# Softmax units bound for a DMA transpose keep their exponentials in PSUM and are split from there

## The chip, the cores and the metric

The kernel runs on one core of a Trainium2 chip. The metric is the device time of one execution in microseconds (us). Five engines have queues of their own: TensorE (PE in the profile; PEld is its weight load), VectorE (DVE), ScalarE (ACT), GpSimd (POOL) and SyncE (SP), which here issues all DMA transfers.

## The reference

Two residual layers on x of 1024 tokens by 1024 columns. Each layer norms x, projects it once, runs three mixers on the parts, multiplies each by its SiLU gate, projects the concatenation back and adds it to x.

```python
for layer in range(2):
    h = rms_norm(x, ln_g[layer])
    if layer % 2 == 0:
        u = h @ even_w_in[0]
        y1 = mla_mixer(...) * silu(a_gate)      # 8 heads, causal softmax over 1024 keys
        y2 = nsa_mixer(...) * silu(b_gate)      # 8 heads; compressed, all earlier and last 512 keys
    else:
        u = h @ odd_w_in[0]
        y1 = dsa_mixer(...) * silu(c_gate)      # 8 heads; softmax over the 256 keys an indexer picks
        y2 = mlstm_mixer(...) * silu(d_gate)    # matrix memory, no softmax
    y_m = mem_xattn(...)                        # 4 heads, softmax over 256 memory slots
    x = x + concat(y1, y2, y_m * silu(m_gate)) @ w_out[layer]
```

Every softmax is exp(s - max s), its sum, and the product with V divided by that sum.

## The kernel before

**The planner.** No engine's order is written out by hand. The kernel is recorded as a list of operations on virtual tiles. `places` gives each operation a due key from the segment that it belongs to (the table `SEG`: start and end key) and makes one order by key, as far as dependencies and room for tiles allow. `order` then deals the operations out to the engines by list scheduling with modelled costs (`time_of`), modelled hand-over times (`LAT`) and the room in four SBUF pools and eight PSUM banks (`LIMITS`: "pg" 30 pages of 4 KB, "hp" 32 of 2 KB, "B" 8 banks). An operation recorded with alternatives (`rec.flex`) goes to the engine that would finish it first by the model. The order that comes out is fixed in the program; the chip keeps it, engine by engine.

A segment's key counts only against other work that is ready at the same time: `mem1` (the second memory attention) has keys far below its neighbours and still waits for the projection that makes its queries.

**The attention units.** `attention` cuts each mixer's softmax into units of one tile of 128 queries and one to four heads: up to 512 score columns in one unit, or one head where a head alone has more. A unit goes through these steps:

- `u_S`: matmuls write the scores to one or two PSUM banks (two beyond 512 columns). DVE takes the row maximum, negated, into `nm`. Then ln 2048 (`lnp`) is added to `nm`, on DVE or POOL. For the masked dsa units one DVE instruction adds the mask, writes the sum to an SBUF page `smask` and returns the maximum; negation and ln 2048 are one more DVE instruction.
- `u_exp`: one ACT instruction for each head reads the scores (PSUM, or `smask`), adds `nm`, takes the exponential, writes fp32 to an SBUF page `P` and sums the row into `rs`. The row's largest value is so 2048.
- Then one of two ways to the transposed fp16 pair that PV takes. A unit with `turn` is split in SBUF by `u_split`: high half `PS[:,0]` = fp16(P), a flex copy for ACT or DVE; low half `PS[:,1]` = P - high, a flex subtraction for DVE or POOL. One DMA transpose then moves both halves to `PT`. A unit without `turn` is transposed by TensorE in fp32 (`psum<-cst,P`), and ACT copies the high half and DVE subtracts the low half out of PSUM (`u_T`, `u_lo`).
- `u_PV`: three matmuls for each block of 128 keys, high and low halves of P and V.

`TURN` sets which units turn: half of mla and nsa, all of mem, three quarters of dsa.

**Stages of the profiled run.** 0 to 300 us: start and even projections. 300 to 850: mla, nsa and the first memory attention among the rest of the projections. 850 to 1200: output projection of layer 0, odd projections, the search for the top 256 keys. 1200 to 1365: second memory attention, mLSTM and the end of the search. 1365 to 1549: dsa and the last output projections.

All recorded instructions show line L558 (the place where `issue` emits them), so the profile is read by tile names.

Of the kernel before, what the change touches and what calls it, by code (L numbers as in the profile page):

```python
# [8 lines left out]
F = mybir.dt.float32  # L9
R = mybir.dt.float32r  # L10
BF = mybir.dt.bfloat16
H = mybir.dt.float16
I32 = mybir.dt.int32
AF = mybir.ActivationFunctionType
OP = mybir.AluOpType
# [618 lines left out]
NEG = -1e30  # L634
EPS = 1e-6
NT = 8
LNP = float(np.float32(11 * np.log(2.0)))
SPLIT = 3
LIMITS = {"pg": 30, "hp": 32, "t8": 32, "t32": 8, "B": 8}

# [21 lines left out]
def shape_constants():  # L662
# [8 lines left out]
    for i in range(NT):  # L671
# [5 lines left out]
    return c  # L677


SEG = dict(setup=(-540.765888, -490.733443), norm=(12.964708, 132.050679), e_agate=(31.455813, 704.234339), kv0=(167.224773,  # L680
           345.119047), late=(175.636113, 461.177491), nsak=(275.848244, 1055.795764), q1=(476.701035, 603.438676),
           cmp=(484.672636, 639.334256), nsav=(624.336051, 851.116142), e_kv1=(652.6, 653.6), e_lat=(663.1, 841.289575),
           e_bgate=(688.806149, 749.106149), q0=(713.750502, 956.450502), kv1=(725, 935.4), e_bq=(743.2, 988.9), e_mq=(762.470888,
           932.2), e_kv2=(794.4, 841.5), nsa=(850.7, 1310.2), tab1=(897.605545, 1585.900938), mla0=(911.5, 1001.5), mla1=(952.8,
           1035.2), mem1=(1004.344435, 1330.229828), oA0=(1007.9, 1178.4), mkv0=(1037.7, 1137.062), mem0=(1060.581418, 1262.6),
           oBM0=(1118.8, 1360.2), o_idx=(1297.169979, 1412.178903), topk0=(1312.341201, 1905.3), o_og1=(1334.12618, 1624.221757),
           o_cgate=(1379.576354, 1777.449577), topk1=(1430.809671, 1885.899198), o_og0=(1492.923662, 1808.788497),
           o_mq=(1651.070557, 1759.482667), o_cq=(1677.868104, 1840.650339), o_dqk=(1707.761464, 1804.647378), mlstm=(1753.080505,
           2015.6), o_dv=(1790.7, 1900.9), mkv1=(1795.03316, 1858.78446), oBM1=(1913.5, 2201.9), cv=(1942.975868, 2132.206114),
           dsa=(1984.716978, 2256.916978), oA1=(2154.023358, 2441.25515))  # L690


LOENG = "GV"
UNIT = 512
NMENG = "GV"
# [8 lines left out]
class Trunk:  # L704
# [88 lines left out]
    def setup(self):  # L793
        V, S, G, T, Q, A = self.V, self.S, self.G, self.T, self.Q, self.A
        cst = self.const([128, C_F32], F, "cst")
        Q.dma_start(cst, A["cst"][:, 0:C_F32])
        self.cst = cst
        self.idf = cst[:, C_ID:C_ID + 128]
        self.gcol = gcol = self.const([128, GCOL], F, "gcol")
        Q.dma_start(gcol, A["cols"])  # L800
        self.nhalf = self.const([128, 32], F, "nhalf")
        V.memset(self.nhalf, -0.5)
        self.lnp = self.const([128, 4], F, "lnp")
        V.memset(self.lnp, LNP)
        self.half = self.const([128, 8], F, "half")
        V.memset(self.half, 0.5)
        self.ones = self.const([128, 128], F, "ones")
        V.memset(self.ones, 1.0)
        self.gmax = self.const([128, 6], F, "gmax")
        self.gcols = {}  # L810
        cols = self.tiny(6, F, "gcm")
        for j, (nm, o, n) in enumerate((("ln0", 0, 8), ("ln1", 8, 8), ("mem0", 16, 8), ("mem1", 24, 8), ("qlat", 32, 2), ("kvlat", 34, 1))):
            self.gcols[nm] = (gcol[:, o:o + n], self.gmax[:, j:j + 1])
            V.tensor_reduce(out=cols[:, j:j + 1], in_=gcol[:, o:o + n], axis=AX.X, op=OP.max, apply_absolute_value=True)
        self.gcols[None] = (None, 1.0)
        gm = self.spread(cols, 6)
        V.tensor_copy(self.gmax, gm)
        V.tensor_tensor(out=self.gmax, in0=self.gmax, in1=self.gmax, op=OP.mult)
# [288 lines left out]
    def v_scale(self, views, nh, c=1):  # L1107

        V = self.V
        m = self.tiny(nh, F, "vm")  # L1110
        for n, v in enumerate(views):
            P = v.shape[0]
            dst = m if n == 0 else self.tiny(nh, F, "vm2")
            if n == 0 and P < 128:
                V.memset(m, 0.0)
            V.tensor_reduce(out=dst[0:P], in_=v, axis=AX.X, op=OP.max, apply_absolute_value=True)
            if n:
                V.tensor_tensor(out=m[0:P], in0=m[0:P], in1=dst[0:P], op=OP.max)
        e = self.tile([128, 3, 8], F, "t32", "vsc")
        V.tensor_scalar(e[:, 0, 0:nh], self.spread(m, nh), 1e-30, None, op0=OP.max)  # L1120
        V.tensor_scalar(e[:, 0, 0:nh].bitcast(I32), e[:, 0, 0:nh].bitcast(I32), 0x7F800000, None, op0=OP.bitwise_and)
        V.tensor_scalar(e[:, 1, 0:nh].bitcast(I32), e[:, 0, 0:nh].bitcast(I32), -1.0, float(268 << 23), op0=OP.mult, op1=OP.add)
        V.tensor_scalar(e[:, 2, 0:nh].bitcast(I32), e[:, 0, 0:nh].bitcast(I32), float((14 + c) << 23), None, op0=OP.subtract)
        return e[:, 1, 0:nh], e[:, 2, 0:nh]

    def v_split(self, v, scale, hi, lo):
# [35 lines left out]
    def u_S(self, u):  # L1162
        T, V = self.T, self.V
        g = u["grp"]
        n, st = u["n"], u["st"]
        per = len(u["heads"])
        s = u["s"] = self.psS(1 if per * st <= 512 and n <= 512 else 2)
        k = min(len(u["heads"]), max(1, 512 // st))
        banks = [[], []]
        for j, h in enumerate(u["heads"]):  # L1170
            for x, (c0, c1) in enumerate(self.cuts(n)):
                b, o = (x, 0) if n > 512 else (j // k, j % k * st)
# [15 lines left out]
                T.matmul(o, l, r, start=(x == 0), stop=(x == len(mm) - 1))  # L1188
        nm = u["nm"] = self.tiny(per, F, "nm")
        if g.get("addmask") is not None:  # L1190
            sm = u["sm"] = self.page("smask")
            for j in range(per):
                V.tensor_tensor_reduce(out=self.like(sm[:, j * n:(j + 1) * n], n), in0=self.head(u, j),
                                       in1=self.like(g["addmask"], n), scale=1.0,
                                       scalar=-3e38, op0=OP.add, op1=OP.max, accum_out=nm[:, j:j + 1])
            V.tensor_scalar(nm, nm, -1.0, LNP, op0=OP.mult, op1=OP.add)
            return
        elif n > 512:
            V.tensor_reduce(out=nm, in_=self.span(s, n).unsqueeze(1), axis=AX.XY, op=OP.max, negate=True)
        elif k > 1:  # L1200
            nb = per // k
            sv = s[:, :, 0:k * st].rearrange("p b (h c) -> p b h c", h=k)[:, :, :, 0:n]
            V.tensor_reduce(out=nm.rearrange("p (b h) -> p b h", b=nb), in_=sv, axis=AX.X, op=OP.max, negate=True)
        else:
            V.tensor_reduce(out=nm, in_=s[:, :, 0:n], axis=AX.X, op=OP.max, negate=True)
        self.tt(nm, nm, self.lnp[:, 0:per], OP.add, NMENG)

    def head(self, u, j):
        n, st, s = u["n"], u["st"], u["s"]
# [3 lines left out]
        return s[:, j // k, j % k * st:j % k * st + n]  # L1213

    def u_exp(self, u):
        g = u["grp"]
        n, st = u["n"], u["st"]
        p = u["p"] = self.page("P", [128, n * len(u["heads"])])
        for j, h in enumerate(u["heads"]):
            src = self.like(u["sm"][:, j * n:(j + 1) * n], n) if "sm" in u else self.head(u, j)  # L1220
            self.S.activation(self.like(p[:, j * n:(j + 1) * n], n), src, AF.Exp, bias=u["nm"][:, j:j + 1], scale=1.0,
                              accum_out=g["rs"][:, h:h + 1])

    def u_split(self, u):

        if not u["turn"]:
            return
        n = u["n"] * len(u["heads"])
        ps = u["ps"] = self.page("PS", [128, 2, n], H)
        p = u["p"][:, 0:n]  # L1230
        self.copy(ps[:, 0], p)
        self.tt(ps[:, 1], p, ps[:, 0], OP.subtract, LOENG)

    def u_T(self, u):
        n = u["n"] * len(u["heads"])
        nb = n // 128
        pt = u["pt"] = self.page("PT", [128, 2, nb, 128], H)
        if u["turn"]:
            self.turn(pt.rearrange("p f k c -> p (f k) c"), u["ps"].rearrange("p f c -> p (f c)"))
            return  # L1240
        p = u["p"]
        u["tt"] = []
        for b0 in range(0, nb, 4):
            b1 = min(nb, b0 + 4)
            t = self.psT()
            for b in range(b0, b1):
                self.T.transpose(t[:, 128 * (b - b0):128 * (b - b0) + 128], p[:, 128 * b:128 * b + 128], self.idf)
            self.S.activation(pt[:, 0, b0:b1].rearrange("p k c -> p (k c)"), t[:, 0:128 * (b1 - b0)], AF.Copy)
            u["tt"].append((b0, b1, t))

    def u_lo(self, u):
        pt = u["pt"]
        for b0, b1, t in u.get("tt", []):
            f = lambda x: pt[:, x, b0:b1].rearrange("p k c -> p (k c)")
            self.V.tensor_tensor(out=f(1), in0=t[:, 0:128 * (b1 - b0)], in1=f(0), op=OP.subtract)

    def u_PV(self, u):
        g, pt, T = u["grp"], u["pt"], self.T
# [1207 lines left out]
```

## Time and profile before

| | |
|---|---|
| median of 3 runs | 1545.11 us (1543.31 to 1551.86) |
| the profiled execution | 1550.77 us, its span 1548.9 us |
| mean granted TensorE clock | 0.956 of full speed |
| busy in the span | PE 1392.3, DVE 1378.1, ACT 1048.5, POOL 419.7 us |

Busy time sums the durations of an engine's instructions. PE's are modelled and overlap, so its share is an upper reading. The median lies 5.66 us under the profiled execution, which has 1.9 us outside its span.

### The profile page before, as it was taken

Reading aid. Unit: us, or ns where it says so; the run is one execution under the profiler, and the core shown is the slowest. Engines: PE = TensorE matmul, PEld = TensorE weight load, DVE = VectorE, ACT = ScalarE, POOL = GpSimd, SP = SyncE. Lnnn points to the kernel's source line nnn. Section 1 sums busy time; section 2 is a strip of 40 time slices with the busy share of each in tenths; the row PEclk is TensorE's granted clock in tenths of the full one; section 3 lists DMA queues with packets and bytes.
Section 4 is the critical chain, followed back from the end, with each engine's and each line's share of the span. In section 5 each row is a group of like instructions: output and inputs, shape, how many; then the busy total and the mean of one; then the engine's idle time right before and its main releaser. Section 6 shows DMA issues by size and latency. Waiting matters only on the chain.

```text
span 1548.9 us, 30286 instructions
## 1 busy us (share of the span) xinstructions
PE 1392.3 (90%) x10407; PEld 797.4 (51%) x10407; DVE 1378.1 (89%) x3813; ACT 1048.5 (68%) x2498; POOL 419.7 (27%) x527
## 2 busy tenths in 40 slices
PE   4999999978888778969889999999989879998988
PEld 1445546545556655546555554444444455656544
DVE  7765989999999988899889999999999989798994
ACT  7633775576767777786686689999875763466650
POOL 1311244546633242243323200003330212121220
PEclk9999999989999999989999999999998867699999
DMA  9826522367496798979997413201431285299995
GB/s 289 195 75 172 158 71 93 88 150 159 100 179 114 156 183 236 220 138 205 209 235 174 108 48 131 81 25 51 123 109 51 62 181 133 74 207 235 212 232 162
DMA packets 441850, 225.49 MB, mean 146 GB/s; under 512 B 378080, under 2 KB 404320, under 8 KB 441696
## 3 DMA queue, kind: packets, MB, share of 16 engines
q1 hardware_dynamic: 441696, 223.57, 61.0%
q8 instruction: 81, 1.33, 0.4%
q14 instruction: 73, 0.60, 0.1%
HBM read 83.61 MB, written 46.66 MB: 84 GB/s over the span
## 4 chain that ended last, share of the span: by engine, by line
PE 31%; DVE 13%; DMA 4%; issue 2%; ACT 1%; POOL 0%; SPq 0%; ACTq 0%; DVEq 0%
PE psum L558 31%; DMA PT<-PS 3%; DVE tkj L558 1%; DVE nm L558 1%; DVE smask L558 1%; DVE PS L558 1%; DVE wl L558 1%; DVE tkp L558 1%; DVE osp L558 1%; DVE row L558 1%; DVE tke L558 0%; DVE PT L558 0%; DMA oT<-osp 0%; DMA gate<-gate_d 0%; DVE x L558 0%
## 5 line engine op out<-in xcount | busy, mean ns | idle before, releaser
L558 PE MATMUL psum<-wl,hT 128*128 128x512 f16 (+3 forms) x2880 | 669.0, 374 | 11.2 <-DMA hT<-nh 4.0
L558 PEld LDWEIGHTS <-hT 128*128 128x128 f16 x2880 | 280.2, 99 | 315.9 <-issue 36.4
L558 PE MATMUL psum<-wl,oT 128*128 128x512 f16 x960 | 266.3, 382 | 5.7 <-DVE mixM L558 1.9
L558 PEld LDWEIGHTS <-PT 128*128 128x128 f16 x3792 | 223.7, 102 | 92.0 <-DMA PT<-PS 50.7
L558 ACT ACTIVATE P<-psum,nm 128x256 f32<-128x256 f32 (+8 forms) x336 | 191.8, 582 | 90.9 <-POOL nm L558 37.2
L558 POOL TENSOR_TENSOR ms<-ms,nhalf 128x4 f32<-128x4 f32 (+3 forms) x105 | 114.2, 1097 | 430.6 <-DVE ms L558 261.4
L558 PE MATMUL psum<-nv,PT 128*128 128x64 f16 x1584 | 174.8, 195 | 19.6 <-DMA PT<-PS 16.7
L558 DVE TENSOR_REDUCE nm<-psum 128x2 f32<-128x512 f32 (+8 forms) x216 | 162.9, 764 | 16.7 <-PE psum L558 16.4
L558 ACT ACTIVATE tkj<-tkj 128x512 bf16<-128x512 bf16 (+5 forms) x192 | 149.9, 783 | 17.2 <-DVE tkj L558 13.0
L558 PEld LDWEIGHTS <-oT 128*128 128x128 f16 x960 | 93.2, 99 | 102.5 <-issue 6.9
L558 DVE TENSOR_TENSOR PS<-P,PS 128x512 f16<-128x512 f32 (+6 forms) x138 | 116.8, 849 | 1.3 <-ACT PS L558 1.2
L558 PE MATMUL psum<-cst,P 128*128 128x128 f32 x502 | 102.8, 292 | 13.2 <-ACT P L558 9.1
L558 PEld LDWEIGHTS <-qf 128*128 128x128 f16 x832 | 77.6, 103 | 49.3 <-issue 15.2
L558 ACT ACTIVATE wj<-wr 128x1024 bf16<-128x1024 f32 (+4 forms) x76 | 77.7, 1024 | 27.8 <-DMA wr<-w_out 16.7
L558 ACT ACTIVATE PT<-psum 128x512 f16<-128x512 f32 (+3 forms) x160 | 76.5, 504 | 29.3 <-PE psum L558 21.7
L558 PE MATMUL psum<-nkst,qf 128*128 128x320 f16 (+5 forms) x384 | 90.2, 319 | 5.8 <-DVE PT L558 2.5
L558 DVE TENSOR_TENSOR wl<-wr,wl 128x1024 f16<-128x1024 f32 (+3 forms) x79 | 93.7, 1190 | 1.8 <-ACT wl L558 1.6
L558 DVE TENSOR_TENSOR PT<-psum,PT 128x512 f16<-128x512 f32 (+3 forms) x160 | 88.1, 566 | 2.0 <-ACT PT L558 1.7
L558 PE MATMUL psum<-cvp,PT 128*128 128x64 f16 x864 | 70.9, 195 | 13.1 <-DMA PT<-PS 10.1
L558 PEld LDWEIGHTS psum<-cst,P 128*128 128x128 f32 x502 | 65.7, 142 | 32.0 <-ACT P L558 13.6
L558 PE MATMUL psum<-vp,PT 128*128 128x64 f16 x864 | 65.3, 197 | 11.9 <-DMA PT<-PS 6.7
L558 POOL TENSOR_TENSOR nm<-nm,lnp 128x1 f32<-128x1 f32 (+2 forms) x116 | 30.6, 265 | 149.1 <-DVE nm L558 133.2
(494 smaller groups left out, 2894.0 us busy)
## 6 DMA issues: line engine op xcount, KB each, us to landing
wr<-even_w_in SPq DMA_DIRECT2D x20, 512.0 KB, 6.0
wr<-w_out SPq DMA_DIRECT2D x20, 512.0 KB, 5.1
wr<-odd_w_in SPq DMA_DIRECT2D x20, 512.0 KB, 4.9
gate<-gate_d SPq DMA_DIRECT2D x32, 256.0 KB, 3.8
gate_d<-gu SPq DMA_DIRECT2D x24, 256.0 KB, 2.2
qa_d<-mqT SPq DMA_DIRECT2D x16, 384.0 KB, 2.4
xt<-x SPq DMA_DIRECT2D x8, 512.0 KB, 10.3
x<-x SPq DMA_DIRECT2D x8, 512.0 KB, 4.7
```

The costliest lines, as they stand in the source:

```text
L558: r = getattr(engines[o.eng], meth)(*[res(a) for a in args], **{k: res(v) for k, v in kw.items()})
```

## The change

1. `lnp` and the addition of ln 2048 to `nm` are gone, so exponentials reach 1 and not 2048. The factor comes back as `PSCALE` = 2048 where the fp16 halves are made: `scale=PSCALE` on the high copy, and a `scalar_tensor_tensor` (in0 x 2048 - high) for the low half. For units without `turn` these are the same two instructions out of PSUM with a factor in them. The constants of `v_scale` undo the factor in the row sums.
2. A unit with `turn` has no page `P`: ACT writes the exponentials over the scores in PSUM, and both halves are made from there. The low half can then only be DVE's (`sub` with a factor names DVE alone). The high copy stays a choice of ACT and DVE.
3. The masked dsa scores go back into their PSUM banks and not to `smask`; this page is gone for all dsa units with a mask.
4. Of the 42 segments of the `SEG` table 35 have new keys. Those that move most (start to end key): `nsak` 276-1056 to 515-835, `kv0` 167-345 to 79-407, `late` 176-461 to 108-589, `norm` 13-132 to 34-47, `cmp` 485-639 to 385-672, `o_mq` 1651-1759 to 1595-1695, `o_cq` 1678-1841 to 1736-1892, `cv` 1943-2132 to 1846-2069, `oBM1` 1914-2202 to 1962-2217, `mem1` 1004-1330 to -818-279.

```diff
-LNP = float(np.float32(11 * np.log(2.0)))
+PSCALE = 2048.0
...
-        self.lnp = self.const([128, 4], F, "lnp")
-        V.memset(self.lnp, LNP)
...
-            sm = u["sm"] = self.page("smask")
             for j in range(per):
-                V.tensor_tensor_reduce(out=self.like(sm[:, j * n:(j + 1) * n], n), in0=self.head(u, j),
-                                       in1=self.like(g["addmask"], n), scale=1.0,
+                V.tensor_tensor_reduce(out=self.head(u, j), in0=self.head(u, j), in1=self.like(g["addmask"], n), scale=1.0,
                                        scalar=-3e38, op0=OP.add, op1=OP.max, accum_out=nm[:, j:j + 1])
-            V.tensor_scalar(nm, nm, -1.0, LNP, op0=OP.mult, op1=OP.add)
-            return
+            V.tensor_scalar(nm, nm, -1.0, None, op0=OP.mult)
...
-        self.tt(nm, nm, self.lnp[:, 0:per], OP.add, NMENG)
...
     def u_exp(self, u):
-        p = u["p"] = self.page("P", [128, n * len(u["heads"])])
+        if not u["turn"]:
+            u["p"] = self.page("P", [128, n * len(u["heads"])])
         for j, h in enumerate(u["heads"]):
-            src = self.like(u["sm"][:, j * n:(j + 1) * n], n) if "sm" in u else self.head(u, j)
-            self.S.activation(self.like(p[:, j * n:(j + 1) * n], n), src, AF.Exp, bias=u["nm"][:, j:j + 1], scale=1.0,
-                              accum_out=g["rs"][:, h:h + 1])
+            src = self.head(u, j)
+            dst = src if u["turn"] else self.like(u["p"][:, j * n:(j + 1) * n], n)
+            self.S.activation(dst, src, AF.Exp, bias=u["nm"][:, j:j + 1], scale=1.0, accum_out=g["rs"][:, h:h + 1])
...
     def u_split(self, u):
-        p = u["p"][:, 0:n]
-        self.copy(ps[:, 0], p)
-        self.tt(ps[:, 1], p, ps[:, 0], OP.subtract, LOENG)
+        n, per = u["n"], len(u["heads"])
+        ps = u["ps"] = self.page("PS", [128, 2, n * per], H)
+        k = min(per, max(1, 512 // u["st"]))
+        if n > 512 or per == 1:
+            src, f = self.head(u, 0), lambda x: self.like(ps[:, x], n)
+        else:
+            src = u["s"][:, :, 0:k * u["st"]].rearrange("p b (h c) -> p b h c", h=k)[:, :, :, 0:n]
+            f = lambda x: ps[:, x].rearrange("p (b h c) -> p b h c", b=per // k, h=k)
+        self.copy(f(0), src, scale=PSCALE)
+        self.sub(f(1), src, f(0), scale=PSCALE)
...
-            self.S.activation(pt[:, 0, b0:b1].rearrange("p k c -> p (k c)"), t[:, 0:128 * (b1 - b0)], AF.Copy)
+            self.S.activation(pt[:, 0, b0:b1].rearrange("p k c -> p (k c)"), t[:, 0:128 * (b1 - b0)], AF.Copy, scale=PSCALE)
...
-            self.V.tensor_tensor(out=f(1), in0=t[:, 0:128 * (b1 - b0)], in1=f(0), op=OP.subtract)
+            self.sub(f(1), t[:, 0:128 * (b1 - b0)], f(0), scale=PSCALE)
```

## Rows read from the trace of the kernel before

**Rows 1.** Windows: us, busy us (instructions) by engine, granted clock, DMA share, GB/s

```profile
300.00:850.00 550.00, 464.86 (x5036) 309.79 (x5034) 512.16 (x1248) 398.19 (x1039) 210.15 (x306) 0.97 0.82 173
850.00:1200.00 350.00, 344.40 (x1638) 165.16 (x1636) 334.97 (x905) 293.61 (x643) 58.13 (x54) 0.98 0.28 83
1200.00:1365.00 165.00, 143.43 (x780) 86.18 (x779) 145.45 (x413) 90.72 (x250) 30.09 (x29) 0.76 0.47 117
1365.00:1549.00 184.00, 165.00 (x1558) 95.72 (x1557) 151.22 (x412) 91.73 (x203) 31.04 (x31) 0.98 0.94 210
```

**Rows 2.** The page, chain that ended last, share of the span by engine

```profile
PE 31%; DVE 13%; DMA 4%; issue 2%; ACT 1%; POOL 0%; SPq 0%; ACTq 0%; DVEq 0%
```

**Rows 3.** Waits of PE, 300 to 850 us: total us, times, longest us

```profile
PE psum L558 <- DMA PT<-PS: 28.4, 19, 5.0
PE psum L558 <- ACT P L558: 19.4, 26, 2.2
PE psum L558 <- DVE PT L558: 16.0, 22, 1.7
```

**Rows 4.** Waits of ACT, 300 to 850 us

```profile
ACT P L558 <- POOL nm L558: 32.3, 28, 3.2
```

**Rows 5.** Groups by shape: the additions to nm on DVE (busy us, mean ns)

```profile
L558 DVE TENSOR_TENSOR nm<-nm,lnp 128x1 f32<-128x1 f32 x61 | 11.2, 184 | 0.2
L558 DVE TENSOR_TENSOR nm<-nm,lnp 128x2 f32<-128x2 f32 x29 | 4.5, 154 | 0.0
L558 DVE TENSOR_TENSOR nm<-nm,lnp 128x4 f32<-128x4 f32 x10 | 2.0, 201 | 0.0
```

**Rows 6.** Timeline around 448 us: start us, us, instruction

```profile
447.36 0.95 DVE L558 TENSOR_REDUCE nm<-psum 128x1 f32<-128x768 f32 x1
...
448.39 0.19 POOL L558 TENSOR_TENSOR nm<-nm,lnp 128x1 f32<-128x1 f32 x1 [2.37 <-DVE nm L558]
...
448.61 0.90 ACT L558 ACTIVATE P<-psum,nm 128x768 f32<-128x768 f32 x1
...
449.63 0.84 ACT L558 ACTIVATE PS<-P 128x768 f16<-128x768 f32 x1
...
450.92 1.65 POOL L558 TENSOR_TENSOR PS<-P,PS 128x768 f16<-128x768 f32 x1
```

**Rows 7.** Windows of tile PS alone: busy us (instructions) DVE, ACT, POOL

```profile
300.00:850.00 550.00, 107.24 (x146) 31.02 (x47) 20.86 (x15) 0.97 0.82 173
1200.00:1365.00 165.00, 16.18 (x29) 5.03 (x8) 0.00 (x0) 0.76 0.47 117
1365.00:1549.00 184.00, 40.61 (x57) 9.41 (x12) 10.95 (x7) 0.98 0.94 210
```

**Rows 8.** Windows of tile nm alone: busy us (instructions) DVE, ACT, POOL

```profile
300.00:850.00 550.00, 161.93 (x276) 185.72 (x576) 29.44 (x112) 0.97 0.82 173
1200.00:1365.00 165.00, 15.69 (x39) 20.31 (x80) 0.39 (x2) 0.76 0.47 117
```

**Rows 9.** The page's groups: the low halves on DVE (busy us, mean ns)

```profile
L558 DVE TENSOR_TENSOR PS<-P,PS 128x512 f16<-128x512 f32 (+6 forms) x138 | 116.8, 849 | 1.3 <-ACT PS L558 1.2
```

**Rows 10.** Groups by shape on DVE, 512 columns (mean ns)

```profile
L558 DVE TENSOR_TENSOR PS<-P,PS 128x512 f16<-128x512 f32 x54 | 41.2, 766 | 0.6 <-ACT PS L558 0.5
L558 DVE TENSOR_TENSOR PT<-psum,PT 128x512 f16<-128x512 f32 x92 | 62.0, 682 | 1.4 <-ACT PT L558 1.3
L558 DVE CAST PS<-P 128x512 f16<-128x512 f32 x34 | 16.1, 474 | 0.5 <-ACT P L558 0.5
L558 DVE TENSOR_SCALAR gu<-psum,winv 128x512 f32<-128x512 f32 x8 | 6.0, 744 | 0.0
```

**Rows 11.** Groups by shape on ACT, 512 columns (mean ns)

```profile
L558 ACT ACTIVATE PT<-psum 128x512 f16<-128x512 f32 x92 | 54.2, 595 | 24.1 <-PE psum L558 17.3 <-DVE PS L558 3.7 <-DMA PT<-PS 2.4
L558 ACT ACTIVATE PS<-P 128x512 f16<-128x512 f32 x28 | 17.8, 635 | 0.4
```

**Rows 12.** Windows of tile smask alone: busy us (instructions) DVE, ACT

```profile
1365.00:1549.00 184.00, 41.22 (x47) 45.83 (x96) 0.98 0.94 210
```

More of the change, by code (lines that the diff above doesn't have):

```diff
@@ L677, in shape_constants @@
     return c
[L680 to L690, printed above, removed]
@@ new lines @@
+SEG = dict(setup=(-887.176746, -575.014179), mem1=(-818.104608, 279.148712), e_agate=(30.064605, 726.188487), norm=(33.814806,
+           46.567053), kv0=(79.294457, 406.744216), late=(107.887518, 589.489146), cmp=(384.926552, 672.131649), q1=(486.699749,
+           566.879955), nsak=(515.461903, 834.75308), nsav=(539.37667, 851.116142), e_kv1=(647.207588, 648.207588), e_lat=(663.1,
+           841.289575), q0=(716.011325, 958.711325), e_bgate=(717.414855, 765.602334), kv1=(721.080648, 931.480648), e_bq=(743.2,
+           988.9), e_mq=(765.062608, 934.79172), e_kv2=(784.700952, 841.5), nsa=(850.7, 1310.2), tab1=(907.178297, 1568.867316),
+           mla0=(911.5, 1001.5), mla1=(949.844544, 1032.244544), oA0=(1017.297313, 1145.595371), mkv0=(1037.7, 1137.062),
+           mem0=(1060.562837, 1262.240461), oBM0=(1119.643991, 1371.691747), o_idx=(1293.212411, 1403.388382), topk0=(1314.820916,
+           1927.025474), o_og1=(1332.958304, 1623.288011), o_cgate=(1393.498171, 1809.325093), topk1=(1431.703909, 1887.435987),
+           o_og0=(1537.324563, 1830.06217), o_mq=(1595.039309, 1695.130732), o_dqk=(1707.756033, 1804.641946), o_cq=(1735.958173,
+           1892.235555), mlstm=(1752.857474, 2015.6), o_dv=(1790.7, 1900.9), mkv1=(1795.03316, 1858.78446), cv=(1845.919745,
+           2068.562291), oBM1=(1961.877043, 2217.498363), dsa=(1968.250395, 2289.566052), oA1=(2185.072731, 2442.45093))
@@ L1119, in v_scale @@
         e = self.tile([128, 3, 8], F, "t32", "vsc")
-        V.tensor_scalar(e[:, 0, 0:nh], self.spread(m, nh), 1e-30, None, op0=OP.max)
+        V.tensor_scalar(e[:, 0, 0:nh], self.spread(m, nh), 1e-29, None, op0=OP.max)
         V.tensor_scalar(e[:, 0, 0:nh].bitcast(I32), e[:, 0, 0:nh].bitcast(I32), 0x7F800000, None, op0=OP.bitwise_and)
         V.tensor_scalar(e[:, 1, 0:nh].bitcast(I32), e[:, 0, 0:nh].bitcast(I32), -1.0, float(268 << 23), op0=OP.mult, op1=OP.add)
-        V.tensor_scalar(e[:, 2, 0:nh].bitcast(I32), e[:, 0, 0:nh].bitcast(I32), float((14 + c) << 23), None, op0=OP.subtract)
+        V.tensor_scalar(e[:, 2, 0:nh].bitcast(I32), e[:, 0, 0:nh].bitcast(I32), float((25 + c) << 23), None, op0=OP.subtract)
         return e[:, 1, 0:nh], e[:, 2, 0:nh]
@@ L1216, in u_exp @@
         g = u["grp"]
-        n, st = u["n"], u["st"]
-        p = u["p"] = self.page("P", [128, n * len(u["heads"])])
+        n = u["n"]
+        if not u["turn"]:
+            u["p"] = self.page("P", [128, n * len(u["heads"])])
         for j, h in enumerate(u["heads"]):
-            src = self.like(u["sm"][:, j * n:(j + 1) * n], n) if "sm" in u else self.head(u, j)
-            self.S.activation(self.like(p[:, j * n:(j + 1) * n], n), src, AF.Exp, bias=u["nm"][:, j:j + 1], scale=1.0,
-                              accum_out=g["rs"][:, h:h + 1])
+            src = self.head(u, j)
+            dst = src if u["turn"] else self.like(u["p"][:, j * n:(j + 1) * n], n)
+            self.S.activation(dst, src, AF.Exp, bias=u["nm"][:, j:j + 1], scale=1.0, accum_out=g["rs"][:, h:h + 1])
     def u_split(self, u):
@@ L1227, in u_split @@
             return
-        n = u["n"] * len(u["heads"])
-        ps = u["ps"] = self.page("PS", [128, 2, n], H)
-        p = u["p"][:, 0:n]
-        self.copy(ps[:, 0], p)
-        self.tt(ps[:, 1], p, ps[:, 0], OP.subtract, LOENG)
+        n, per = u["n"], len(u["heads"])
[8 more added lines that the diff above has]
+        self.sub(f(1), src, f(0), scale=PSCALE)
     def u_T(self, u):
```

## The prediction

> **What bounds the kernel now.** I read the windows by stage first. In the attention stage, 300 to 850 us, DVE is busy 512.2 of 550 us (93%), PE 464.9 (85%), ACT 398.2 (72%) and the DMA engines 0.82 of the time; from 850 to 1200 PE is busy 344.4 of 350; from 1200 to 1365 the granted clock is only 0.76 with DVE at 88%; in the dsa stage DVE is at 82%, PE at 90%, the DMA engines at 0.94 [rows 1]. So the change lands in three stages and in none does one engine do everything. The chain of work that ended last says the same: 31% of the span on PE, 13% on DVE, 4% on DMA [rows 2]. In the attention stage PE waits 28.4 us for transposed pairs, 19.4 us for exponentials and 16.0 us for low halves out of PSUM [rows 3]. The reader is to see that DVE is the fullest there, but that a third of what PE waits for is the transpose behind it.
>
> **1. The addition of ln 2048 goes.** On DVE 61 + 29 + 10 = 100 additions take 11.2 + 4.5 + 2.0 = 17.7 us, 0.177 us each [rows 5]. In the attention stage tile nm has 276 instructions on DVE and 112 on POOL; one addition goes with each maximum, so DVE has (276 - 112)/2 = 82 additions: -14.5 us. From 1200 to 1365 it has (39 - 2)/2, some 18: -3.3 us [rows 8]. The dsa mask units keep their one small instruction. Beside the work a hand-over goes: around 448 us the maximum ends at 448.31, POOL's addition runs to 448.58, the exponential starts at 448.61 [rows 6], so a unit loses 0.3 us there and without POOL perhaps 0.1. ACT ended 28 waits on such an addition, 32.3 us in all [rows 4], but most of each is the maximum that came late. At 0.2 us for the 26 times that PE waited for an exponential [rows 3] the hand-over is worth 5 us at most; I take -2.
>
> **2. The low half moves to PSUM and wholly to DVE.** 138 on DVE took 116.8 us, 849 ns each [rows 9]. At 512 columns the same subtraction is 766 ns from SBUF and 682 ns from PSUM (the low half after a TensorE transpose) [rows 10]. That row has no factor; the third operation of the new instruction runs in the same pass, and the nearest row with a factor from PSUM, a copy with a pointer, is 744 ns, which is the upper end. I take 849 x 682/766 = 756 ns. POOL's share comes over.
>
> **3. The high copy.** From SBUF DVE needs 474 ns at 512 columns, ACT 635; from PSUM ACT needs 595 [rows 10, 11] and DVE, by the subtraction's row, 682. DVE was the cheaper place and becomes the dearer one, so the planner will give ACT more. In the attention stage tile PS has 146 instructions on DVE, 47 on ACT, 15 on POOL: 208, so 104 units, with 104 - 15 = 89 low halves and 57 copies on DVE [rows 7]. Before, DVE had 57 of 104; I take a third, 35, after. The Trainium skill, "VectorE: DVE Perf Modes", section "Why PSUM operands drop a tier", says that a PSUM operand costs a DVE copy its double rate in fp32; the trace agrees, 474 against 682 ns. Its section "Rules for kernel authors" goes on that many operations on a matmul's output want a copy to SBUF first, which is what the old kernel did: by that rule the change loses (rival D).
>
> **DVE by stage.** Attention: 104 low halves and 35 copies x 0.756 = 105.1 us against 107.2 now [rows 7]; with the additions -16.6. Bounds: all 57 copies stay, 161 x 0.756 = 121.7, sum 0.0; all leave, 78.6, sum -43. From 1200 to 1365: 37 instructions, 18.5 units of 512 columns, 18.5 + 6 at 0.682 = 16.7 against 16.2; with the additions -2.8. Dsa: (57 + 12 + 7)/2 = 38 units, now 40.6 us on DVE [rows 7]. They are wider: the masking of one such unit out of PSUM takes 41.22/47 = 0.877 us [rows 12], so 38 + 13 operations are 44.7 us: +4.1. Bounds: no copy on DVE, 33.3, -7.3; the present 57 - 31 = 26 stay, 56.1, +15.5.
>
> **ACT and POOL.** In the attention stage ACT takes 22 copies more, at 31.02/47 = 0.66 less 0.04 us: +14, to 75% busy; that has room. POOL loses its 20.9 + 29.4 us [rows 7, 8] and was the bound nowhere.
>
> **4. Writing to PSUM.** No row has ACT or DVE write there. For ACT's exponentials and DVE's masking I take the present price; the bounds are the two sides of what another place of a source makes, 40 ns on ACT and 84 ns on DVE at 512 columns [rows 10, 11]: within 4 us of DVE work for the 47 masked heads, and ACT has room. The masked exponentials read PSUM in place of SBUF, which by the same 40 ns saves 2 us of ACT.
>
> **5. Banks are held longer.** A turned unit now gives its scores' bank back when the exponential ends, at 449.51 in the example; afterwards when the low half is made. The copy there ran from 449.63 to 450.47 and the subtraction (POOL's, begun at 450.92) needs some 0.9 us on DVE [rows 6]: some 2 us longer, in two banks beyond 512 columns. 104 units x 2 us x 1.5 banks = 312 of 8 x 550 = 4400 bank-us, 7%. Below: nothing, if the planner finds another bank; above: rival C. I take +1 us. The Trainium skill, "ScalarE: Activation LUTs", section "Step-by-step: what each stage is for", calls PSUM the faster destination for ScalarE, useful only if TensorE does not need most of it. No row here shows such a write; the caveat is rival C.
>
> **6. Pages.** Up to 160 `P` pages and 48 masks are no longer allocated; that lets later units start earlier. No price shows; I count nothing, and the upside is in rival B.
>
> **7. The new keys.** Each moved segment issues the same instructions and DMAs; what changes is whom they are queued in front of, SP's transfers included. `kv0`, `late` and `norm` bring weight and table loads forward behind the first x tiles; `cv` brings its transpose of keys and three DVE instructions ahead of `oBM1`; `o_mq` passes `o_cq`, so the second memory attention can begin earlier, and cq's stores wait. From 850 to 1200 PE is at 344.4 of 350 us, so no order there can win more than 5.6. From 1200 to 1365 there is more: 143.4 us of PE work at clock 0.76 [rows 1] would be some 109 at full clock, so up to -34. A wrong order costs by the same measure. `mem1` was far ahead of its neighbours already and its new key changes nothing. I take 0 in the middle, +-15.
>
> **The sum.** Of 16.6 us less DVE work in the attention stage I let three fifths, 10, reach the end, since PE's 28.4 us for transposes stay. Hand-over -2; 1200 to 1365 -1; dsa +2 (half of 4.1, as DVE is at 82%); banks +1: -10 us. The profiled execution's 1550.77 us would be 1540.8; it lies 5.66 us above the median of the runs, so against 1545.11 I predict 1535.
>
> **The rivals.**
> A. Nothing changes: PE and the transposes set the end. For it: the chain, and PE's longest wait [rows 2, 3]. Against: DVE at 93%. Within 5 us of 1545.
> B. More than forecast: units run ahead on the freed pages, half of PE's 19.4 us for exponentials goes (-10), and the new order wins a third of the 34 us at the low clock (-11). With the -10: 1514.
> C. Banks: score matmuls wait for a bank until the low half is made. 10 us over 104 units is 0.1 us a unit; from there the gain is gone. At 0.25 us a unit it is +26 - 10: 1561. For it: 7% more bank time and PE's 16.0 us for low halves out of PSUM; against: the order is planned with the banks.
> D. The copies stay on DVE: 0 in the attention stage, half of 15.5 in dsa: 1553.
>
> **Chances.** Forecast 0.42 (its own range 1527 to 1541), A 0.20, B 0.16, C 0.12, D 0.10. Less than 0.5% (7.7 us) can't be told from no change. Faster by more: 0.36 of the forecast's 0.42, all of B, a trace of A: 0.53. Slower: C, half of D, a little of A: 0.19. The same: 0.28. From 1508 to 1560 leaves out about half of B's faster end and two thirds of C, under 2 in 10 together.
>
> **What would show it.** No nm addition on POOL; the exponential a hand-over behind the maximum. PS rows: 160 low halves on DVE near 756 ns, under 60 copies on DVE, over 100 on ACT. DVE in the attention stage some 15 us lower. Under C, PE waits in front of score matmuls (psum<-Kn, nkst, ckst) for DVE PS or ACT PS, where none stand now. Wrong it would be if the clock between 1200 and 1365 moves far from 0.76, which the keys can do and no term here sizes, or if DVE's idle time grows as much as its work shrinks.

## The result, and the profile after

Over four runs the new kernel's median is 1530.78 us (1522.73 to 1536.33); before, beside it, 1545.78. The ratio is 0.9891, 95% interval 0.9858 to 0.9924: 1.1% faster, where the prediction gave 1535. The profiled execution took 1530.51 us, span 1528.7; before, 1548.9. So the two traces differ by 20.2 us, 5 more than the medians.

Windows by stage, new kernel (columns as in [rows 1]):

```profile
300.00:850.00 550.00, 475.17 (x5088) 313.78 (x5087) 508.38 (x1162) 414.17 (x1072) 171.87 (x205) 0.97 0.79 176
850.00:1200.00 350.00, 338.80 (x1623) 163.94 (x1620) 338.21 (x901) 293.82 (x645) 43.70 (x42) 0.98 0.27 80
1200.00:1365.00 165.00, 148.18 (x874) 90.03 (x873) 154.87 (x440) 94.10 (x273) 44.82 (x46) 0.79 0.54 126
```

The attention stage has 10 us more of PE's work in the same 550 us, and DVE is nearly as full as before (508.38 against 512.16 us), though tiles nm and PS alone cost it 18 us less: work moved forward into the stage. ACT's 16 us more are the high copies that it took over (48.18 against 31.02 us on tile PS). The chain that ended last reaches back to 44.94 us here. That of [rows 2] reaches back only to 753.71 us, so its shares add up to about half of the span, and the two can't be compared:

```profile
PE 47%; DVE 33%; DMA 7%; issue 5%; ACT 3%; POOL 1%; SPq 0%; DVEq 0%; POOLq 0%; ACTq 0%
```

Windows of tile PS (first three lines: attention, 1200 to 1365, dsa; DVE, then ACT), and of tile nm (last line, attention), which answer to [rows 7, 8]:

```profile
300.00:850.00 550.00, 103.42 (x136) 48.18 (x72) 0.97 0.79 176
1200.00:1365.00 165.00, 22.85 (x37) 10.86 (x19) 0.79 0.54 126
1365.00:1529.00 164.00, 31.93 (x33) 18.91 (x23) 1.00 0.94 224
...
300.00:850.00 550.00, 147.67 (x194) 189.95 (x576) 0.97 0.79 176
```

POOL is gone from both tiles. Tile PS by operation (count: shortest/median/longest ns, over the whole run):

```profile
L558 DVE SCALAR_TENSOR_TENSOR PS<-psum,PS x160: 409/682/1225, 324.6 to 1493.2; 128x512 f16<-128x512 f32 x62, 128x640 f16<-128x640 f32 x30, 128x384 f16<-128x384 f32 x18, 128x768 f16<-128x768 f32 x14
...
L558 ACT ACTIVATE PS<-psum x114: 374/643/1046, 320.2 to 1491.9; 128x512 f16<-128x512 f32 x40, 128x640 f16<-128x640 f32 x19, 128x384 f16<-128x384 f32 x15, 128x768 f16<-128x768 f32 x11
L558 DVE TENSOR_SCALAR PS<-psum x46: 418/682/1224, 337.1 to 1464.9; 128x512 f16<-128x512 f32 x22, 128x640 f16<-128x640 f32 x11, 128x384 f16<-128x384 f32 x3, 128x896 f16<-128x896 f32 x3
```

Waits of PE, 300 to 850 us, to be held against [rows 3]:

```profile
PE psum L558 <- DVE PS L558: 21.3, 24, 3.2
PE psum L558 <- DMA PT<-PS: 15.8, 16, 3.3
PE psum L558 <- DVE PT L558: 9.9, 15, 1.8
PE psum L558 <- ACT P L558: 5.9, 10, 1.8
```

The first line is new: matmuls that wait until a bank's low half is made. The other three fell from 28.4 + 19.4 + 16.0 = 63.8 us to 31.6; with the new one it is 52.9.

**Where the 20.2 us arose.** The tile views give the start of the last matmul of a kind. The last nsa product with V (`psum<-nv,PT`) starts at 845.6 us before and at 838.2 after: 7.4 us. The first exponential came at 308.7 and comes at 304.9, so 3.8 of these lie ahead of it and 3.6 behind it. But before, an addition on POOL stood in front of that exponential, so part of the change's own gain lies ahead of this landmark. The first row maximum starts at 304.6 and 303.5: counted from it, 1.1 lie ahead of the attention and 6.3 in it. The last projection matmul (`psum<-wl,hT`) starts at 1299.9 and 1281.9: a further 10.6 us between the two landmarks. From there to the end it is 249.0 and 246.8: 2.2 us. Windows of the middle stretch, before and then after:

```profile
845.60:1299.90 454.30, 429.74 (x2176) 214.31 (x2174) 430.96 (x1158) 355.66 (x815) 76.82 (x74) 0.94 0.33 93
```

```profile
838.20:1281.90 443.70, 420.14 (x2180) 210.82 (x2179) 427.77 (x1133) 352.60 (x814) 71.88 (x76) 0.96 0.34 95
```

PE issues the same matmuls there, and its idle time is 24.6 and 23.6 us. 9.6 of the 10.6 us are matmul time, at a granted clock of 0.94 against 0.96. Slices of 10 us show where. Before:

```profile
1150.00:1160.00 10.00, 6.17 (x32) 3.06 (x29) 10.00 (x24) 9.95 (x21) 1.58 (x2) 0.98 0.67 182
1160.00:1170.00 10.00, 9.69 (x22) 3.68 (x23) 9.66 (x16) 6.70 (x17) 0.21 (x1) 0.51 0.47 105
1170.00:1180.00 10.00, 10.00 (x23) 2.83 (x21) 9.64 (x10) 3.27 (x4) 0.00 (x0) 0.66 0.00 0
...
1250.00:1260.00 10.00, 7.21 (x66) 4.97 (x65) 10.00 (x28) 8.86 (x31) 0.74 (x3) 0.50 1.02 199
...
1270.00:1280.00 10.00, 10.00 (x61) 6.31 (x60) 7.26 (x26) 3.91 (x9) 1.01 (x1) 0.50 0.90 306
```

PE was busy 6.17 of 10 us, and in the next slice it has 1.2 GHz (0.51) and gets through 22 matmuls where the slices around have some 50. Between 1100 us and the last projection matmul four slices of before are at 0.57 or less; the new kernel has none there (its next is at 0.50, from 1290 us, behind that matmul), the lowest being this one:

```profile
1230.00:1240.00 10.00, 5.77 (x39) 3.65 (x39) 10.00 (x22) 8.14 (x32) 0.60 (x3) 0.59 0.95 160
```

So half of the difference between the two traces lies where few turned units run. The experiments ask what belongs to the code and what to the order of its work.

### The profile page after: what moved, and what is told of

Same layout as the page of the kernel before. It is cut to its first block, busy times and chain, and to the rows that moved or that the text cites. A ratio compares the mean times of both kernels' runs of the same rounds, so it can differ in the third digit from the quotient of the medians.

```text
span 1528.7 us, 29963 instructions
## 1 busy us (share of the span) xinstructions
PE 1386.7 (91%) x10407; PEld 793.7 (52%) x10407; DVE 1375.7 (90%) x3683; ACT 1066.5 (70%) x2527; POOL 375.4 (25%) x413
## 4 chain that ended last, share of the span: by engine, by line
PE 47%; DVE 33%; DMA 7%; issue 5%; ACT 3%; POOL 1%; SPq 0%; DVEq 0%; POOLq 0%; ACTq 0%
PE psum L558 47%; DMA PT<-PS 6%; DVE nm L558 5%; DVE PS L558 4%; DVE tkj L558 3%; DVE wl L558 3%; DVE PT L558 2%; DVE cy L558 1%; DVE score L558 1%; DVE psum L558 1%; POOL ms L558 1%; DVE mixB L558 1%; DMA xp_d<-x 1%; DVE qs L558 1%; DVE wr L558 1%
## 5 line engine op out<-in xcount | busy, mean ns | idle before, releaser
L558 PE MATMUL psum<-wl,oT 128*128 128x512 f16 x960 | 274.2, 386 | 8.6 <-DVE PS L558 3.2
L558 ACT ACTIVATE tkj<-tkj 128x640 bf16<-128x640 bf16 (+5 forms) x192 | 149.8, 782 | 39.5 <-DVE tkj L558 30.9
L558 ACT ACTIVATE psum<-psum,nm 128x256 f32<-128x256 f32 (+8 forms) x234 | 137.1, 590 | 54.3 <-DVE nm L558 39.9
L558 DVE SCALAR_TENSOR_TENSOR PS<-psum,PS 128x512 f16<-128x512 f32 (+6 forms) x160 | 123.7, 782 | 2.2 <-ACT PS L558 2.0
L558 ACT ACTIVATE P<-psum,nm 128x64 f32<-128x64 f32 (+8 forms) x150 | 92.5, 625 | 37.6 <-DVE nm L558 27.4
L558 DVE SCALAR_TENSOR_TENSOR PT<-psum,PT 128x512 f16<-128x512 f32 (+3 forms) x160 | 87.9, 566 | 9.0 <-ACT PT L558 8.6
L558 ACT ACTIVATE wj<-wr 128x1024 bf16<-128x1024 f32 (+6 forms) x78 | 79.2, 1016 | 19.2 <-DMA wr<-even_w_in 7.5
L558 DVE TENSOR_TENSOR wl<-wr,wl 128x1024 f16<-128x1024 f32 (+4 forms) x75 | 90.8, 1219 | 1.3 <-ACT wl L558 1.1
L558 PE MATMUL psum<-cvp,PT 128*128 128x64 f16 x864 | 81.6, 193 | 7.2 <-DMA PT<-PS 6.5
L558 ACT ACTIVATE PS<-psum 128x512 f16<-128x512 f32 (+6 forms) x114 | 78.0, 686 | 2.0 <-PE psum L558 0.3
```

The lines of the kernel that those rows point to most:

```text
L558: r = getattr(engines[o.eng], meth)(*[res(a) for a in args], **{k: res(v) for k, v in kw.items()})
```

## The experiments

Runs are compared by their ratio to the kernel before, measured beside them. A difference of two such ratios, times 1545.8, is given in us; the new kernel's own ratio, 0.9891, is uncertain by 5 us.

**Keys and code apart.** e1 is the old code with the new table, e2 the new code with the old one.

```diff
-SEG = dict(setup=(-541..., ...), ...)   # e1: in the old code
+SEG = dict(setup=(-887.176746, -575.014179), mem1=(-818.104608, 279.148712), ...)
```

> The kernel before with nothing changed but the key table of the new one. Theory A (the code makes the gain: less DVE work and no hand-over through POOL): ratio to the kernel before 0.997 to 1.003. Theory B (the key table makes it): 0.985 to 0.992, and most of it after 850 us, where the new kernel's last hT matmul comes 18 us earlier while its attention stage (first exponential to last nv product) is only 3.6 us shorter. Theory C (the order that the planner happens to find makes it): anywhere from 0.99 to 1.01.

> The new kernel with the old key table. Theory A: 0.987 to 0.993, all of the gain. Theory B: 0.997 to 1.005. If both parts add up, the product of this ratio and that of the run with the new keys alone is 0.989.

e1: 1589.52 us, ratio 1.0284 (1.0251 to 1.0317). e2: 1559.81, 1.0105 (1.0076 to 1.0135). Each is slower than both kernels, so neither part alone makes the old kernel faster.

**Keys moved by nothing that means anything.** If a table fits its own code, a small random shift should cost. In e3 (old code) and e4 (new code) each pair of keys is shifted by a random amount of at most 1, on a scale of some 3,000.

```diff
-nsa=(850.7, 1310.2), ...
+nsa=(851.590541, 1311.090541), ...   # e3; each segment its own shift
```

> The kernel before, each segment's key pair shifted by a random amount within 1 (of some 2400): no meaning in it, so it measures what an arbitrary new order is worth. Theories A and B: 0.997 to 1.003. Theory C: a shift as large as the gain itself, 0.5% or more either way.

> The new kernel with its key pairs shifted in the same way within 1. Theories A and B: 0.986 to 0.992 as the new kernel itself. Theory C: it loses half of the gain or more, 0.994 or above.

e3: 1573.67 us, 1.0187 (1.0163 to 1.0210): 29 us slower than before. e4: 1559.07, 1.0094 (1.0071 to 1.0118): 31 us slower than the new kernel. Both tables stand on a narrow peak. An order found for one code costs about as much on another as one found for none, so e1 and e2 say little by themselves about keys or code: each lost its own peak.

**The code on keys chosen for neither.** e5 is the new code on e3's keys. A second shift gives the pair e9 (old code) and e10 (new code).

> The new code with the shifted old keys of the run before_keys_shifted (1573.7 us), so that neither code has a table sought out for it. If the code is worth what it is worth between the two tuned kernels, 10 to 20 us less: ratio to the kernel before 1.005 to 1.012. If the code is worth nothing and the two tables differ by luck: 1.014 to 1.022. If more than between the tuned kernels: under 1.005.

> Before's code; each old pair of keys moved by a second random amount of at most 1. With e10 it is a second pair on keys chosen for neither code (the first was e3 and e5, 1573.7 and 1570.5 us). Theory 1 (what a key table is worth to its own code is larger than what the change of code is worth): slower than before by 15 to 45 us, 1560 to 1590. Rival (the 28 us of e3 were bad luck with one table): within 8 us of 1546.

> The new code with the keys of e9. Theory 1 as in e3 and e5: the two differ by under 10 us in either direction. Rival (the code is worth its 15 us on any keys, and the first pair hid it): 12 us or more below e9.

| keys | old code | new code | difference |
|---|---|---|---|
| first shift: e3, e5 | 1.0187 | 1.0170 (1.0133 to 1.0208) | -0.2%, 3 us |
| second shift: e9, e10 | 1.0243 (1.0205 to 1.0281) | 1.0136 (1.0093 to 1.0178) | -1.1%, 17 us |
| last nsa product with V, e3, e5 | 869.8 us | 862.1 us | -7.7 us |
| the same, e9, e10 | 872.5 us | 853.5 us | -19.0 us |

e9 repeats what a shift costs, 38 us. The pairs differ by 3 and 17 us, some 10 us with an uncertainty nearly as large. What I held after the first pair, that the code is worth less than 10 us, fell with the second. The attention stage is what holds up: on both tables it ends earlier with the new code, by 8 and 19 us. Counted from the first row maximum (306.8 and 305.8 us in e3 and e5, 304.7 and 303.7 in e9 and e10) it is 6.7 and 18.0 us shorter. In the first pair some 5 us of that were given back later.

All untuned orders together say more than the two pairs. The new code has four of them (e2, e4, e5 and e10), with ratios from 1.0094 to 1.0170 and a mean of 1.0126. The old code has three (e1, e3 and e9), from 1.0187 to 1.0284, mean 1.0238. No order of the old code is as fast as the slowest of the new one (though e3 and e5 differ by less than their uncertainty), and the means differ by 1.1%, 17 us, which is about what the two tuned kernels show. With orders that differ among themselves by 12 and 15 us this stays an estimate.

**The exponentials out of PSUM again.** e6 keeps the new kernel's issued order instruction for instruction, but 152 of its 160 turned units write their exponentials to one of up to three SBUF places (`ring`) and both halves are made from there. The other eight found no place free and stay in PSUM.

```diff
-activation(dst, src, AF.Exp, ...)                       # dst: the scores' bank
+activation(ring, src, AF.Exp, ...)                      # where a place is free
-copy(f(0), src, scale=PSCALE); sub(f(1), src, f(0), scale=PSCALE)
+copy(f(0), ring, scale=PSCALE); sub(f(1), ring, f(0), scale=PSCALE)
```

> The new kernel in its own order of instructions, but with the exponentials of 152 of the 160 turned units written to three places in SBUF and both halves made from there (8 units find no place free and stay in PSUM). Banks theory (holding the scores' banks until the low half is made costs PE the 28.7 us that it waits for DVE PS from 300 to 1365 us): 8 to 20 us faster than the new kernel, ratio to before 0.976 to 0.984. Rival (those waits only take the place of others, and PSUM as a source makes up for them): within 5 us of the new kernel, 0.986 to 0.992, low halves near 850 ns and DVE copies near 480 ns. If three places are too few, slower, with ACT waiting for DVE PS.

1551.14 us, 1.0044 (1.0024 to 1.0064): 24 us over the new kernel in the same order (20 between the medians). Tile PS of e6:

```profile
L563 DVE SCALAR_TENSOR_TENSOR PS<-ring,PS x152: 407/813/3146, 324.0 to 1513.6; 128x512 f16<-128x512 f32 x61, 128x640 f16<-128x640 f32 x30, 128x384 f16<-128x384 f32 x18, 128x768 f16<-128x768 f32 x12
...
L563 DVE TENSOR_SCALAR PS<-ring x44: 283/442/1395, 336.5 to 1485.9; 128x512 f16<-128x512 f32 x22, 128x640 f16<-128x640 f32 x11, 128x384 f16<-128x384 f32 x3, 128x1024 f16<-128x1024 f32 x3
```

DVE is busy 1395.7 us against 1375.7. The copies get cheaper (483 against 678 ns at 512 columns). The low halves get dearer, the longest 3146 ns against 1225, but not at every one of them. At 512 columns the 34 that had no POOL instruction beside them took 682 ns in the mean, against 680 for such ones from PSUM in the new kernel. The 27 with POOL beside them took 1064 in the mean and up to 2435; from PSUM such ones took 677. Over all 152, by the start and duration of each, the low halves cost 25.7 us more than the same shapes from PSUM in the new kernel, and 25.5 us of that lie in the 61 with POOL beside them. The same POOL instruction with a low half beside it, in e6 and then in the new kernel:

```profile
674.89 2.13 POOL L563 TENSOR_TENSOR wl<-wr,wl 128x1024 f16<-128x1024 f32 x1 [2.92 <-ACT wl L563]
675.37 2.20 DVE L563 SCALAR_TENSOR_TENSOR PS<-ring,PS 128x512 f16<-128x512 f32 x1
```

```profile
603.29 2.14 POOL L558 TENSOR_TENSOR wl<-wr,wl 128x1024 f16<-128x1024 f32 x1 [4.44 <-ACT wl L558]
604.16 0.81 DVE L558 SCALAR_TENSOR_TENSOR PS<-psum,PS 128x640 f16<-128x640 f32 x1
```

From SBUF the low half ended 0.55 us after POOL's instruction did; from PSUM it took its usual time. The waits of e6 show that the banks are free again:

```profile
PE psum L563 <- DVE PT L563: 24.2, 30, 3.2
PE psum L563 <- DMA PT<-PS: 17.8, 17, 3.4
PE psum L563 <- ACT P L563: 15.2, 17, 2.9
...
PE psum L563 <- ACT ring L563: 9.7, 9, 2.3
```

PE waits 2.5 us for DVE PS where the new kernel has 28.7, and longer for what DVE and ACT make. Held banks are thus the cheaper side in this order, but e6 pays two prices for SBUF beside the banks that it frees: the 25.5 us of DVE beside POOL, and the small ring, as ACT waits 17.9 us for a low half to free a place. It doesn't show what freed banks are worth by themselves.

**The hand-over of the maximum.** e7 puts a POOL addition behind each of the 216 maxima in the new kernel's order, as the old code had one on DVE or POOL. It adds -0.5, so that exponentials are smaller by a constant factor, which their sum has too. e12 makes the same addition into a tile that nobody reads. e8 leaves the additions out of the old kernel in its own order, so that its exponentials reach 1.

```diff
 V.tensor_reduce(out=nm, in_=s[:, :, 0:n], ..., op=OP.max, negate=True)
+G.tensor_tensor(out=nm, in0=nm, in1=nhalf, op=OP.add)     # e7
+G.tensor_tensor(out=sink, in0=nm, in1=nhalf, op=OP.add)   # e12
-self.tt(nm, nm, self.lnp[:, 0:per], OP.add, NMENG)        # e8, in the old kernel
```

> The new kernel in its own order of instructions, with one addition on POOL put back behind each of the 216 maxima (-0.5 in place of ln 2048, the same in every exponential of a row, so it falls out of the quotient). My term (the hand-over was worth 2 us, 5 at most): ratio to before 0.990 to 0.993. Rival (it is on the path in most of the 113 waits of ACT for a maximum, at 0.3 us or more): over 20 us slower than the new kernel, 1.002 or above.

> The kernel before in its own order of instructions, with the 216 additions of ln 2048 left out when the instructions are emitted (exponentials reach 1 and not 2048, so the low halves lose some bits; the rest is as before). By my terms: 17.7 us of DVE work and a hand-over go, 5 to 12 us, ratio 0.992 to 0.997. If the fixed order lets nothing through: 0.998 to 1.000. If the hand-over is dear: 0.990 or less.

> As e7, the new kernel in its own issued order with one POOL addition behind each of the 216 maxima, but its result goes to a tile of its own that nobody reads, so that no exponential waits for it. The same load on POOL without the hand-over. Theory (the 20 us of e7 are the hand-over on the way to the exponential, 216 times some 0.3 us, a third of which reaches the end): within 4 us of the new kernel, 1527 to 1535. Rival (POOL's load itself, by what it delays on POOL or by its accesses beside DVE's): 1540 or more.

e7: 1550.72 us, 1.0036 (1.0017 to 1.0056), 22 us over the new kernel. e12: 1541.96, 0.9967 (0.9944 to 0.9990), 12 us over it. So in this order 11 us (e7 less e12) go with the hand-over and 12, uncertain by 6, with the additions' presence on POOL, though no exponential waits for them. Neither of e12's two theories had both. Waits of ACT in e7:

```profile
ACT P L559 <- POOL nm L562: 41.7, 44, 3.5
ACT psum L559 <- POOL nm L562: 38.8, 43, 2.3
```

In e12, the unread additions and what POOL waits for in front of them:

```profile
L562 POOL TENSOR_TENSOR sink<-nm,nhalf x216: 179/190/1220, 305.0 to 1497.5; 128x1 f32<-128x1 f32 x71, 128x2 f32<-128x2 f32 x24, 128x4 f32<-128x4 f32 x13
...
  DVE nm L559: 219.8, 123
```

An instruction of 0.19 us holds POOL's queue until its maximum is there, 219.8 us in all, and what is queued behind it waits too. DVE is not slower for it (1375.4 us busy, 1375.7 in the new kernel). That the queue is how the 12 us come about is argued, not shown. The traces place the two costs differently. The last nsa product starts at 852.4 us in e7 and at 841.9 in e12, so the hand-over's share, 10.5 us, lies up to the end of the attention stage. There e12 is only 3.7 us behind the new kernel, with 194 of the 216 additions done; 6.5 us it loses behind the last projection matmul, where at most 22 additions run. The mean granted clock of the runs is 0.956 in e6, 0.958 in e7 and 0.961 in e12, against 0.962 in the new kernel, and PE is busy 1391.2 us in e6's trace and 1397.9 in e7's against 1386.7, so part of what these two lose is matmul time.

e8: 1541.88 us, 0.9972 (0.9950 to 0.9995): 4 us faster than before. In the old order ACT still comes when it was planned to, and waits for the maximum itself, 85.2 us where before had 57.3 for it and 37.2 for POOL's addition:

```profile
ACT P L563 <- DVE nm L563: 85.2, 64, 5.7
```

**In PSUM, with the addition kept.** e11 takes e3's keys and the new code, but leaves the addition of ln 2048 as it was; the split has the factor 1.

```diff
-PSCALE = 2048.0
+PSCALE = 1.0
+        self.tt(nm, nm, self.lnp[:, 0:per], OP.add, NMENG)   # as in the old code
```

> The keys of e3 and e5; exponentials stay in PSUM as in the new code, but the addition of ln 2048 to nm stays as in the old one, so that the split has no factor (the low half is the same instruction with factor 1). Theory (the two halves of the code need each other: banks held longer are paid for by the addition that is gone): slower than e3 and e5 by 10 us or more, above 1582. Rival (each half is worth its own few us): within 6 us of 1572. The addition's share of DVE alone, 14 us over the kernel at a half to three fifths, would make 7 to 9 us over e5.

1586.28 us, 1.0262 (1.0214 to 1.0310): 12 us above the old code on these keys (e3) and 14 above the new one (e5). That is the gap which the theory named, but the planner makes a third order here, and another order alone has cost 29 to 38 us. Among the untuned orders e11 is slower than all four of the new code (1.0170 at most) and lies within the three of the old (1.0187 to 1.0284). So the gain of the new code is not seen while the addition stays, as far as one order can tell; that exponentials in PSUM are a loss without the other half is not shown. PE's waits for held banks up to the last nsa product, in e11 (300 to 883 us) and then in e5 (300 to 862 us):

```profile
PE psum L558 <- DVE PS L558: 15.3, 15, 4.7
```

```profile
PE psum L558 <- DVE PS L558: 13.2, 23, 1.4
```

ACT's waits for the additions in e11, 300 to 883 us:

```profile
ACT P L558 <- POOL nm L558: 27.4, 22, 4.2
ACT psum L558 <- POOL nm L558: 19.5, 16, 2.8
```

ACT waits 46.9 us for POOL's additions. PE's waits for held banks are hardly longer with the addition than without it, so they don't explain the 14 us.

## Why the prediction was right, and where it was not

The direction and the size came out: 1535 forecast, 1530.8 measured. Part of the agreement is luck, as the steps show.

**1, the addition.** The count and the DVE time are right: tile nm in the attention stage fell from 161.93 to 147.67 us on DVE, 14.3 against 14.5. A maximum that ends at 440.70 us has its exponential start at 440.73, as expected without POOL between them. The hand-over was sized wrongly: -2, "5 us at most", stands against the 11 us between e7 and e12, and POOL's additions go with some 12 more without any hand-over, which the prediction put at nothing (POOL "was the bound nowhere"). The step counted only PE's 26 waits for exponentials. In e7 PE waits 13.6 us for ACT P against 5.6 in e12, and also 37.3 us for low halves against 33.2. In the old order removal is worth only 4 us (e8), so the value depends on an order that uses it.

**2 and 3, the split.** 160 low halves on DVE, as forecast, of 782 ns instead of 756. The step took 766 against 682 ns at 512 columns for the price of the place. The trace of the kernel before says otherwise: there the 35 low halves with no POOL instruction beside them took 680 ns in the mean from SBUF, and the 19 with POOL beside them 924. Over all widths the 53 beside POOL cost 9.4 us more than the same shapes from PSUM in the new kernel, the other 85 only 0.1 us more in all. So the move to PSUM took away what POOL's work did to the low halves, and not a dearer source. The ratio at 512 columns doesn't hold at other widths (1253 against 1216 ns at 1024), which is why 756 was too low. In the new kernel the low halves take 679 ns at 512 columns, and the low half of a TensorE transpose, now with a factor in it, 682, as without [rows 10]:

```profile
L558 DVE SCALAR_TENSOR_TENSOR PT<-psum,PT 128x512 f16<-128x512 f32 x92 | 62.3, 682 | 7.7 <-ACT PT L558 7.5
...
L558 DVE SCALAR_TENSOR_TENSOR PS<-psum,PS 128x512 f16<-128x512 f32 x62 | 41.4, 679 | 0.1
```

So the factor is free, and the excess is not in it. DVE makes 136 - 104 = 32 high copies in the attention stage where I took 35. From 1200 us on, tile PS costs DVE 54.8 us, where the prediction gave 61.4, mostly because the planner moved copies in dsa to ACT too: DVE makes 14 of 56, not 19. For rival D the prediction had named the rule of the Trainium skill, "VectorE: DVE Perf Modes", section "Rules for kernel authors", to copy to SBUF first where many operations follow. e6 puts 152 of the units there and is 24 us slower: the copies do get their speed, but the low half gains nothing from SBUF and is held up there when POOL works beside it.

**4, writes to PSUM.** ACT's exponential into PSUM is 26 ns cheaper than into SBUF at 512 columns, inside the bound of 40. DVE's mask sum is 8 ns dearer at 1024 columns (1224 against 1216 before), and the read of its maximum behind it takes 141 ns in the middle where it took 83; over the 48 masked heads that is 0.5 and 2.8 us, inside the bound of 4:

```profile
L558 ACT ACTIVATE psum<-psum,nm 128x512 f32<-128x512 f32 x18 | 12.0, 666 | 5.6 <-DVE nm L558 5.4
...
L558 ACT ACTIVATE P<-psum,nm 128x512 f32<-128x512 f32 x14 | 9.7, 692 | 4.7 <-DVE nm L558 4.7
```

**5, the banks.** The wait that rival C named is there, 28.7 us in 31 waits over the run, more than the "+1 us" suggests; it took the place of others and did not add to them, so C is not what happened. Nor does e11 show it, since PE waits about as long for held banks there as in e5. The Trainium skill, "ScalarE: Activation LUTs", section "Step-by-step: what each stage is for", was cited for PSUM as the faster destination of ScalarE, useful only where TensorE does not need most of PSUM. The first agrees with 666 against 692 ns; the caveat is not borne out by the new kernel, and no run here shows where it would begin.

**7, the keys.** Here the reasoning failed, though its 0 in the middle hid it. First, keys and code can't be priced apart by one run of each: e1 and e2 are 2.8% and 1.1% slower than before, and shifts that mean nothing cost 29 to 38 us, twice the gain and beyond the "+-15". Secondly, the step bounded the order by PE's idle time between 850 and 1200 and took the clock for a risk of the stretch after. About 10 of the 20.2 us came from matmuls at a higher clock between 1100 and 1282. e6, e7 and e12, which keep the new order, have 421.1, 419.1 and 420.2 us of PE work between those landmarks; e8 keeps the old one and has 427.0 against 429.7. The new code in its other orders (e2, e4, e5 and e10) has 424.9 to 428.9 us, the old code in e1, e3 and e9 422.8 to 428.4. So this part of the gain goes with the order, and not with the code. Which of the 35 moved segments brings it wasn't tried.

**The sum.** Of the 10 us that were to reach the end from the attention stage, the trace at hand shows 6.3 between the first row maximum and the last nsa product; on other keys it is 6.7 and 18.0. The sign that DVE would be some 15 us lower there did not come: it is 3.8 us lower, because other work took the room. More of the 20.2 us came from the middle stretch, 10.6, for which the sum had nothing, so that the forecast of 1535 came so near is partly luck. Rival A is excluded by the interval; B's way (half of PE's waits for exponentials, a third of the low clock) happened in part: these waits went from 19.4 to 5.9 us, and the clock between 1200 and 1365 us rose from 0.76 to 0.79.

**Still open:** whether the new code with as good an order as its own gains more than the old with its own, other than by the 15 us that these two orders show. On keys chosen for neither it is 3 and 17 us, and over all untuned orders some 17. How that divides between the addition, POOL's work and the place of the exponentials is shown for the new order alone, and there the parts (12, 11 and 24 us) add up to more than the whole.

## What to carry to other kernels

When an order is found by search, measure what a meaningless change of its keys does before pricing any edit that comes with a new order: here 2%, more than the edit. A change of code should then be read on the issued order held fixed and on several orders chosen for neither side. A small instruction between two engines is not priced by its duration: 216 of them, of 0.19 us on POOL, went with some 12 us when nobody read their results and with 11 more once the exponentials waited for them. Before a row's mean is taken for the price of a place, look at what ran beside its longest instructions: here the SBUF subtraction's 766 ns at 512 columns were 680 without POOL beside it. Keeping a value in PSUM through its last use paid here, as its subtraction is then not held up by POOL; a slow step between its making and that use may change this, which one order (e11) suggests and doesn't show.

## What the runs showed of the hardware that was not expected

- A factor in DVE's subtraction out of PSUM costs nothing: 682 ns at 512 columns with it and without it.
- ACT is quicker into PSUM than into SBUF with the same source: 666 against 692 ns at 512 columns, in one trace.
- DVE's subtraction with both sources in SBUF (value x factor - high) took 851 ns in the mean at 512 columns in e6, against 679 with the value in PSUM. The whole difference lies with POOL: without a POOL instruction beside it 682 against 680, with one 1064 (up to 2435) against 677. Of the 152 low halves in e6, 31 took over 100 ns more than the same shape from PSUM, and all 31 had POOL beside them. A copy with a factor took 483 from SBUF and 678 from PSUM, so a copy is quicker from SBUF:

```profile
L563 DVE SCALAR_TENSOR_TENSOR PS<-ring,PS 128x512 f16<-128x512 f32 x61 | 51.3, 851 | 1.4 <-ACT PS L563 1.0
...
L563 DVE TENSOR_SCALAR PS<-ring 128x512 f16<-128x512 f32 x22 | 10.6, 483 | 2.7 <-ACT ring L563 2.6
```

- Two slices of 10 us at a granted clock of 0.51 and 0.66 followed one in which PE was busy 6.17 of 10 us; two orders of the same matmuls differ by 9.6 us of PE's busy time in the stretch where such slices lie.
